# Last norm of a one-core transformer block: last quarter summed in PSUM, weights multiplied first, stores cut finer

## The chip, the cores and the metric

The kernel runs on one core of a Trainium2 chip. The metric is device time in microseconds from the start to the end of one execution; lower is better. Three runs of the kernel before took 734.03, 734.28 and 734.59, median 734.28.

## What is computed

A hybrid block on 512 rows of 1024 features: a norm, one wide projection, a gated linear attention branch and a latent attention branch, their gated sum through `w_out`, then a feed-forward part and a last norm. Only the end matters here:

```python
def rmsnorm(x, g):
    y = x * lax.rsqrt(jnp.mean(x * x, axis=-1, keepdims=True) + EPS)
    return y * g
...
m = rmsnorm(h, g_mlp)
h = h + jnp.square(jax.nn.relu(m @ w_ff1)) @ w_ff2     # 512x1024 -> 512x4096 -> 512x1024
return rmsnorm(h, g_final)
```

The output is 512 x 1024 in float32. Each row of the last norm needs the mean square of its whole row of h, so no row can leave before its last part of h is there.

## The kernel before

**Precision.** Every large product is made of three TensorE products: each factor is split into a high part, rounded by ScalarE (`AF.Copy` into a rounded float32 type), and a low part, the rest, which VectorE subtracts. Names end in h and l for the two: `g341h`, `g341l` are weights, `f3h`, `f3l` activations (helper `mm3`: high by high, low by high, high by low).

**Stages.** The feed-forward part runs in four quarters of the 4096 hidden features. Each quarter has a first product (`f0` to `f3`, with `w_ff1`) and a second (`g0` to `g3`, with `w_ff2`). Both are 2 x 2 block products made of seven block products instead of eight, numbered 1, 2, 5, 3, 6, 7, 4 in the order of the second kind. The 512 rows are four row tiles of 128; the tiles `h0` to `h3` (128 x 1024) hold the running h. In the second product, VectorE adds PSUM banks into them (`add_rows`, called by `sink`): `g3x0` and `g3x1` are the banks of blocks 1, 6 and 7 for the upper and lower row tile of a block, `g3z0` and `g3z1` those of 5 and 3. Block 7 adds onto the banks of block 6, so its first product into a bank waits until VectorE has read block 6 out of it.

**The end.** The last block, 4, adds only to the left halves of h2 and h3. `last_rows` makes it as `ge` (row tile 2, 512 columns, 12 products) and then, for row tile 3, as two quarters of 256 columns, `gend0` and `gend1` (12 products each). VectorE adds each into h. Around this the last norm of the four row tiles is made:

- the square of the right half and of the left half (or the two left quarters), on ScalarE, with a row sum into the small tile `hp` (columns 0 and 1); the squares themselves are written into the tile `ms` and not used;
- `out_mean` on GpSimd: sum times 1/D plus EPS; then on VectorE the other sum is added (`hp`, 128x1), and GpSimd takes the power -0.5 (`hp<-hp,mhalf`): this is the factor rs of a row;
- the right half: GpSimd multiplies h by the weights `gfin` into `ms` (`out_gained`), later ScalarE scales it by rs in place (`out_right`);
- the left half: VectorE does both in one instruction (`out_left`);
- `out_store`: two stores of 512 columns, all from the queue of SyncE but the very last, which ScalarE issues.

**What sets the order.** Steps of the earlier phases carry due times. From due time `base + 5700` on, everything is recorded instead of issued (`Held.hold`) and is then emitted in the order of the table `LAST_ROWS` (letter of the engine, tile written, count; P PE, A ScalarE, D VectorE, G GpSimd, S SyncE). Line 76 is where those instructions are emitted, line 90 where the others are; so rows of the end have line 76, and tiles tell them apart. Each engine works through its own queue in order. On GpSimd the queue of the end starts behind the loads of `w_ff2` pieces that it issues (`w<-in_w_ff`).

Of the kernel before, what the change touches and what calls it, by code (L numbers as in the profile page):

```python
# [11 lines left out]
F32 = mybir.dt.float32  # L12
F32R = mybir.dt.float32r
# [5 lines left out]
P = 128  # L19
# [78 lines left out]
def tile_block(ctx: ExitStack, tc: tile.TileContext, t, out: bass.AP):  # L98
# [1676 lines left out]
    def out_first(i):  # L1775
        hparts[i] = sm(f"hp{i}", 4)
        o = u4(f"ms{i}", F32, (P, D))
        ms_rows[i] = o
        nc.scalar.activation(o[:, 0:S], hrow[i][:, S:D], AF.Square, accum_out=hparts[i][:, 0:1])
# [5 lines left out]
    def out_gained(i):  # L1785
        nc.gpsimd.tensor_tensor(ms_rows[i][:, S:D], hrow[i][:, S:D], gains[0][:, S:D], op=ALU.mult)

    def out_square(i, cols, n=1):
        nc.scalar.activation(ms_rows[i][:, cols], hrow[i][:, cols], AF.Square, accum_out=hparts[i][:, n : n + 1])

    def out_rstd(i, n=1):
        p = hparts[i]
        nc.vector.scalar_tensor_tensor(
            p[:, 3:4], p[:, n : n + 1], 1.0 / D, p[:, 2:3], op0=ALU.mult, op1=ALU.add
        )
        nc.gpsimd.tensor_tensor(p[:, 3:4], p[:, 3:4], mhalf, op=ALU.pow)

    def out_left(i):
        o, rs = ms_rows[i], hparts[i][:, 3:4]
        nc.vector.scalar_tensor_tensor(o[:, 0:S], hrow[i][:, 0:S], rs, gains[0][:, 0:S], op0=ALU.mult, op1=ALU.mult)  # L1800

    def out_right(i):
        o, rs = ms_rows[i], hparts[i][:, 3:4]
        nc.scalar.activation(o[:, S:D], o[:, S:D], AF.Copy, scale=rs)

    def out_store(i):
        for c in range(2):
            cols = slice(c * S, (c + 1) * S)
            (nc.scalar if (i, c) == (3, 1) else nc.sync).dma_start(out[0, i * P : (i + 1) * P, cols], ms_rows[i][:, cols])

    def last_rows(ph):

        acc, parts = ps("mm", "ge"), (ps("mm", "gend0"), ps("at", "gend1"))
        cols = [slice(x * HT, (x + 1) * HT) for x in range(2)]

        def last_part(x):
            for p in range(NP):
                ph.second_product(4, parts[x][:, 0:HT], True, 1, p, cols[x])
            nc.vector.tensor_tensor(hrow[3][:, cols[x]], parts[x][:, 0:HT], hrow[3][:, cols[x]], op=ALU.add)

        for p in range(NP):
            ph.second_product(4, acc, True, 0, p)
        for i in (2, 3):
            out_first(i)
        out_mean(2)
        out_mean(3)
        out_gained(2)
        add_rows(2, 0, acc)
        out_square(2, slice(0, S))
# [303 lines left out]
```

## Time and profile before

| | us |
|---|---|
| median of three runs | 734.28 |
| the profiled execution | 733.97 |
| its span, first to last instruction | 732.2 |
| PE busy / VectorE / ScalarE / GpSimd | 723.8 / 624.6 / 494.4 / 223.2 |
| end of PE's last product (725.02 + 0.28) | 725.30 |
| end of the last scale on VectorE (727.48 + 0.75) | 728.23 |
| end of the span | 732.2 |

How to read it: rows of a timeline have the start in us from the begin of the span, the duration, the engine, the line, the operation, what is written and what is read (buffer numbers left out: `h` is any of h0 to h3), and shapes. A bracket at the end is the idle time before the row and who ended it. PE is TensorE, DVE VectorE, ACT ScalarE, POOL GpSimd, SP SyncE. A q behind an engine's name is its queue, as for the issue of a DMA. Matmuls are pipelined, so rows of PE overlap, and so do the first 0.08 us of a DVE row with the row before.

### The profile page before, as it was taken

Reading aid. Unit: us, or ns where it says so; the run is one execution under the profiler, and the core shown is the slowest. Engines: PE = TensorE matmul, PEld = TensorE weight load, DVE = VectorE, ACT = ScalarE, POOL = GpSimd, SP = SyncE. Lnnn points to the kernel's source line nnn. Section 1 sums busy time; section 2 is a strip of 40 time slices with the busy share of each in tenths; the row PEclk is TensorE's granted clock in tenths of the full one; section 3 lists DMA queues with packets and bytes.
Section 4 is the critical chain, followed back from the end, with each engine's and each line's share of the span. In section 5 each row is a group of like instructions: output and inputs, shape, how many; then the busy total and the mean of one; then the engine's idle time right before and its main releaser. Section 6 shows DMA issues by size and latency. Waiting matters only on the chain.

```text
span 732.2 us, 11361 instructions
## 1 busy us (share of the span) xinstructions
PE 723.8 (99%) x4150; PEld 637.6 (87%) x4150; DVE 624.6 (85%) x865; ACT 494.4 (68%) x810; POOL 223.2 (30%) x284
## 2 busy tenths in 40 slices
PE   9999999999999999999999999999999999999996
PEld 7888888888888888888888999889988998899985
DVE  7777887889988897789989789998699869987897
ACT  8556565595686864988867889545873477546855
POOL 0732020243843843226864412200211012101125
PEclk9999999999999999999999999999999999999998
DMA  9848682421222324657958899861987088815863
GB/s 311 279 137 194 214 179 89 82 64 29 58 59 59 90 45 114 180 160 190 246 87 218 188 214 202 177 211 61 249 182 195 11 240 189 199 59 143 173 99 131
DMA packets 81191, 109.93 MB, mean 150 GB/s; under 512 B 16208, under 2 KB 34640, under 8 KB 81136
## 3 DMA queue, kind: packets, MB, share of 16 engines
q1 hardware_dynamic: 63760, 75.64, 32.9%
q0 software_dynamic: 17088, 33.30, 27.5%
q8 instruction: 32, 0.52, 0.3%
q10 hardware_dynamic: 288, 0.28, 0.1%
q14 instruction: 23, 0.19, 0.1%
HBM read 104.22 MB, written 2.10 MB: 145 GB/s over the span
## 4 chain that ended last, share of the span: by engine, by line
PE 96%; DVE 2%; issue 1%; DMA 0%; ACT 0%; POOLq 0%; POOL 0%; DVEq 0%; ACTq 0%
PE f3x L90 3%; PE f2x L90 3%; PE f1x L90 3%; PE f0x L90 3%; PE first L90 3%; PE s L76 3%; PE av L76 3%; PE wox L76 3%; PE g2x L90 3%; PE g1x L90 3%; PE g0x L90 3%; PE gvx L90 3%; PE zax L90 3%; PE grx L90 3%; PE gk L90 2%; PE cq L90 2%
## 5 line engine op out<-in xcount | busy, mean ns | idle before, releaser
L90 POOL DMA_DIRECT2D w<-in_w_ff x32 | 38.6, 1205 | 240.1 <-DMA w<-in_w_ff 139.9
L76 ACT ACTIVATE e<-s,top 128x512 f32<-128x512 f32 x32 | 22.0, 689 | 8.5 <-DVE top L76 7.4
L76 DVE TENSOR_REDUCE top<-s 128x1 f32<-128x512 f32 x32 | 21.6, 685 | 5.9 <-PE s L76 5.6
L76 PE MATMUL s<-kbuf,q 96*128 96x512 f32 x96 | 26.6, 403 | 0.0
L76 PE MATMUL av<-pT,v 128*128 128x512 f32 (+1 forms) x108 | 25.4, 372 | 0.0
L76 DVE TENSOR_TENSOR pT<-tp,pT 128x512 fp32r<-128x512 f32 x32 | 21.7, 685 | 2.3 <-PE s L76 0.9
L76 ACT ACTIVATE pT<-tp 128x512 fp32r<-128x512 f32 x32 | 18.6, 599 | 5.9 <-PE tp L76 5.6
L76 PEld LDWEIGHTS av<-pT,v 128*128 128x128 f32 x108 | 18.6, 189 | 3.3
L76 PEld LDWEIGHTS s<-kbuf,q 96*128 96x128 f32 x96 | 17.0, 189 | 3.1 <-DVE grb L76 0.2
L76 PE MATMUL tp<-ident,e 128*128 128x128 f32 x128 | 17.9, 272 | 0.0
L76 PEld LDWEIGHTS tp<-ident,e 128*128 128x128 f32 x128 | 15.3, 140 | 2.7 <-ACT e L76 0.2
L90 POOL DMA_DIRECT2D gvw<-in_w_in x4 | 4.8, 1230 | 38.7 <-DVE gvw L90 34.0
L90 POOL TENSOR_TENSOR qF<-qk,qF 128x512 fp32r<-128x512 f32 x3 | 5.3, 1759 | 32.7 <-ACT qF L90 32.7
L90 POOL DMA_DIRECT2D zaw<-in_w_in x4 | 4.9, 1228 | 32.7 <-DVE zaw L90 28.0
L90 DVE TENSOR_TENSOR w<-w,w 128x1024 f32<-128x1024 f32 x12 | 14.4, 1221 | 0.1
L76 POOL DMA_DIRECT2D w<-in_w_ff x8 | 9.9, 1355 | 14.9 <-DVE g360l L76 7.0
L76 ACT ACTIVATE ms<-h 128x512 f32<-128x512 f32 (+1 forms) x17 | 10.2, 600 | 4.8 <-DVE h L76 4.7
L90 ACT ACT_TABLE_LOAD x9 | 11.5, 1283 | 1.2 <-PEq L2106 0.8
L76 POOL DMA_DIRECT2D w<-in_w_out x10 | 12.2, 1441 | 0.0
L76 POOL TENSOR_TENSOR my<-tb,yg 128x256 f32<-128x256 f32 x8 | 7.2, 898 | 13.7 <-DVE tb L76 7.5
L76 ACT ACTIVATE e<-e,tot 128x512 f32<-128x512 f32 x16 | 11.3, 720 | 0.0
L76 POOL TENSOR_TENSOR hp<-hp,mhalf 128x1 f32<-128x1 f32 x8 | 7.8, 980 | 8.9 <-DVE hp L76 8.7
(1954 smaller groups left out, 3084.2 us busy)
## 6 DMA issues: line engine op xcount, KB each, us to landing
w<-in_w_ff SPq DMA_DIRECT2D x48, 512.0 KB, 5.4
w<-in_w_ff POOLq DMA_DIRECT2D x40, 512.0 KB, 6.0
w<-in_w_out POOLq DMA_DIRECT2D x10, 512.0 KB, 5.9
grw<-in_w_in SPq DMA_DIRECT2D x8, 512.0 KB, 9.8
zaw<-in_w_in SPq DMA_DIRECT2D x8, 512.0 KB, 7.1
gvw<-in_w_in SPq DMA_DIRECT2D x8, 512.0 KB, 5.3
w<-in_w_out SPq DMA_DIRECT2D x16, 256.0 KB, 3.9
w221f<-in_w_ff SPq DMA_DIRECT2D x8, 512.0 KB, 5.2
```

The lines of the kernel that those rows point to most:

```text
L76: what(*args, **options)
L90: return what(*args, **options)
```

## The change

Four things, all in the last norm:

1. **The last quarter is summed in PSUM.** The right quarter of h3's left half is split into a high and a low part (`hend`, 128 x 2 x 256). Two products of an identity matrix (copied into `ones_r`, which is no longer needed as ones) add the two parts to `gend1`, after the sixth of its twelve products. VectorE's add into h is left out; the square reads the bank.
2. **The weights are multiplied first.** The left halves too get `h * gfin` first and are scaled by rs in place later: for row tiles 0 and 1 on GpSimd, for the two quarters of row tile 3 on VectorE, the last one from the bank. Row tile 2 keeps VectorE's one instruction for its left half.
3. **Who scales.** Left of row tile 0 is scaled by ScalarE, left of row tile 1 by VectorE, both without weights. Row tile 3 is cut at column 640: VectorE scales the 640 left columns, ScalarE the 384 right ones.
4. **Stores.** The right half of row tile 0 and both halves of row tile 1 leave as stores of 256 columns, row tile 3 as 640 and 384. Squares go to a scratch tile `junk`.

```diff
+    def out_begin(i):
+        if not spare:
+            spare.append(u2("junk"))
+            nc.scalar.activation(ones_r, ident, AF.Copy)
...
+    def out_gained(i, cols, eng=nc.gpsimd, src=None):
+        src = hrow[i][:, cols] if src is None else src
+        eng.tensor_tensor(ms_rows[i][:, cols], src, gains[0][:, cols], op=ALU.mult)
+
+    def out_scaled(i, cols, by_vector=False):
+        o, rs = ms_rows[i][:, cols], hparts[i][:, 3:4]
+        if by_vector:
+            nc.vector.tensor_scalar(o, o, rs, None, op0=ALU.mult)
+        else:
+            nc.scalar.activation(o, o, AF.Copy, scale=rs)
...
     def last_rows(ph):
...
+        split(rest[:, 0], rest[:, 1], hrow[3][:, QUARTERS[1]])
         add_rows(2, 0, acc)
...
+        for p in range(NP):
+            ph.second_product(4, last[0], True, 1, p, QUARTERS[0])
+        nc.vector.tensor_tensor(hrow[3][:, QUARTERS[0]], last[0], hrow[3][:, QUARTERS[0]], op=ALU.add)
         out_rstd(2)
+        out_square(3, hrow[3][:, QUARTERS[0]], 1)
+        out_gained(3, QUARTERS[0], nc.vector)
+        for p in range(NP):
+            ph.second_product(4, last[1], True, 1, p, QUARTERS[1])
+            if p == 1:
+                for x in range(2):
+                    nc.tensor.matmul(last[1], ones_r, rest[:, x], start=False, stop=False, skip_group_check=True)
...
+        out_added(3, 1, 2)
+        out_square(3, last[1], 0)
+        out_added(3, 0, 3)
+        out_gained(3, QUARTERS[1], nc.vector, last[1])
+        out_power(3)
+        cut = S + HT // 2
+        out_scaled(3, slice(0, cut), True)
+        out_scaled(3, slice(cut, D))
+        out_store(3, 0, cut)
+        out_store(3, cut, D, nc.scalar)
...
-        step(base + 7000 + i, out_first, i)
-        step(base + 7002 + i, out_mean, i)
-        step(base + 7002 + i, out_gained, i)
+        step(base + 7000 + i, out_begin, i)
+        step(base + 7002 + i, out_gained, i, LEFT)
...
-        A:g361h D:f3l60 P:g3z1*6 D:g361l A:g370h P:g3x1*3 D:f3l61 P:g3x0*3 A:f3h71 G:w2_21 A:f3h41 D:h0 P:g3x0*3
+        A:g361h D:f3l60 P:g3z1*6 D:g361l A:g370h P:g3x1*3 D:f3l61 P:g3x0*3 A:f3h71 G:w2_21 A:ones G:ms0 G:ms1 A:f3h41
```

On GpSimd, the queue behind its last weight load, up to the second row tile's power; `ms` is the tile that is stored, `hp` the small tile with the sums. Before:

```order
L76 DMA w2_21_736_2776<-in_w_ff2 128x2x512
L76 TENSOR_TENSOR ms0_1378_7482<-h0_869_2909,gfin_1330_7321 128x512
L76 TENSOR_SCALAR hp0_1377_7481<-hp0_1377_7481 128x1
L76 TENSOR_TENSOR hp0_1377_7481<-hp0_1377_7481,mhalf_74 128x1
L76 TENSOR_SCALAR hp1_1379_7483<-hp1_1379_7483 128x1
L76 TENSOR_TENSOR ms1_1380_7484<-h1_870_2910,gfin_1330_7321 128x512
L76 TENSOR_TENSOR hp1_1379_7483<-hp1_1379_7483,mhalf_74 128x1
```

And now:

```order
L76 DMA w2_21_736_2776<-in_w_ff2 128x2x512
L76 TENSOR_TENSOR ms0_1379_7483<-h0_869_2909,gfin_1330_7321 128x512
L76 TENSOR_TENSOR ms1_1381_7485<-h1_870_2910,gfin_1330_7321 128x512
L76 TENSOR_TENSOR ms0_1379_7483<-h0_869_2909,gfin_1330_7321 128x512
L76 TENSOR_SCALAR hp0_1378_7482<-hp0_1378_7482 128x1
L76 TENSOR_TENSOR hp0_1378_7482<-hp0_1378_7482,mhalf_74 128x1
L76 TENSOR_SCALAR hp1_1380_7484<-hp1_1380_7484 128x1
L76 TENSOR_TENSOR ms1_1381_7485<-h1_870_2910,gfin_1330_7321 128x512
```

The first two products of 128x512 are new (the left halves of row tiles 0 and 1); everything else stands behind them in the order of before. They wait for nothing later than the end of the `f3` products; the third waits for VectorE's add of block 6 into h0.

On VectorE, from the last split of weights to the end of the queue. Before:

```order
L76 TENSOR_TENSOR h3_872_2912<-h3_872_2912,g3x1_1329_7315 128x512 x2
L76 SCALAR_TENSOR_TENSOR ms0_1378_7482<-h0_869_2909,hp0_1377_7481,gfin_1330_7321 128x512
L76 TENSOR_TENSOR h2_871_2911<-h2_871_2911,ge_1381_7485 128x512
L76 SCALAR_TENSOR_TENSOR ms1_1380_7484<-h1_870_2910,hp1_1379_7483,gfin_1330_7321 128x512
L76 SCALAR_TENSOR_TENSOR hp2_1384_7488<-hp2_1384_7488 128x1
L76 TENSOR_TENSOR h3_872_2912<-gend0_1382_7486,h3_872_2912 128x256
L76 TENSOR_TENSOR h3_872_2912<-gend1_1383_7487,h3_872_2912 128x256
L76 SCALAR_TENSOR_TENSOR ms2_1385_7489<-h2_871_2911,hp2_1384_7488,gfin_1330_7321 128x512
L76 SCALAR_TENSOR_TENSOR hp3_1386_7490<-hp3_1386_7490 128x1 x2
L76 SCALAR_TENSOR_TENSOR ms3_1387_7491<-h3_872_2912,hp3_1386_7490,gfin_1330_7321 128x512
```

And now:

```order
L76 TENSOR_TENSOR h3_872_2912<-h3_872_2912,g3x1_1329_7315 128x512 x2
L76 TENSOR_SCALAR ms1_1381_7485<-ms1_1381_7485,hp1_1380_7484 128x512
L76 TENSOR_TENSOR h2_871_2911<-h2_871_2911,ge_1382_7486 128x512
L76 TENSOR_TENSOR hend_1385_7489<-h3_872_2912,hend_1385_7489 128x256
L76 TENSOR_TENSOR h3_872_2912<-gend0_1383_7487,h3_872_2912 128x256
L76 SCALAR_TENSOR_TENSOR hp2_1386_7490<-hp2_1386_7490 128x1
L76 TENSOR_TENSOR ms3_1389_7493<-h3_872_2912,gfin_1330_7321 128x256
L76 SCALAR_TENSOR_TENSOR ms2_1387_7491<-h2_871_2911,hp2_1386_7490,gfin_1330_7321 128x512
L76 SCALAR_TENSOR_TENSOR hp3_1388_7492<-hp3_1388_7492 128x1 x2
L76 TENSOR_TENSOR ms3_1389_7493<-gend1_1384_7488,gfin_1330_7321 128x256
L76 TENSOR_SCALAR ms3_1389_7493<-ms3_1389_7493,hp3_1388_7492 128x640
```

Row tile 1's left half became a scale, the low half of the split `hend` stands between the add of `ge` and that of `gend0`, and the add of `gend1` gave way to a product with the weights that stands behind the last mean.

On PE, around the place in the last quarter where the two identity products now stand (the same place held none before):

```order
L76 MATMUL gend1_1384_7488<-g340h_1373_7477,f3h40_1322_7295 128x256
L76 MATMUL gend1_1384_7488<-g340l_1374_7478,f3h40_1322_7295 128x256
L76 MATMUL gend1_1384_7488<-g340h_1373_7477,f3l40_1324_7297 128x256
L76 MATMUL gend1_1384_7488<-hend_1385_7489,ones_r_71 128x256 x2
L76 MATMUL gend1_1384_7488<-g341h_1375_7479,f3h41_1323_7296 128x256
L76 MATMUL gend1_1384_7488<-g341l_1376_7480,f3h41_1323_7296 128x256
```

The first of the two waits for ScalarE's high half of `hend`, the second for VectorE's low half; six products of the quarter stand ahead of them and six behind.

More of the change, by code (lines that the diff above doesn't have):

```diff
@@ L1795, in out_rstd, with out_power @@
         )
+    def out_power(i):
+        p = hparts[i]
         nc.gpsimd.tensor_tensor(p[:, 3:4], p[:, 3:4], mhalf, op=ALU.pow)
[L1798 to L1809, printed above, removed]
+    def out_rstd(i):
+        out_added(i, 1, 3)
+        out_power(i)
@@ L1811, in last_rows @@
     def last_rows(ph):
         acc, parts = ps("mm", "ge"), (ps("mm", "gend0"), ps("at", "gend1"))
[L1814 to L1819, printed above, removed]
+        rest = u2("hend", F32R, (P, 2, HT))
         for p in range(NP):
```

85 lines of the change are left out of this document (44 added, 41 removed).

## The prediction

> **What bounds the kernel now.** I read the profile from the whole to the end: first the busy times and the chain that ended last, then a table by stage of the last 18 us, then the rows of each engine there. The page says that TensorE is the bound:
>
> ```profile
> PE 723.8 (99%) x4150; PEld 637.6 (87%) x4150; DVE 624.6 (85%) x865; ACT 494.4 (68%) x810; POOL 223.2 (30%) x284
> PE 96%; DVE 2%; issue 1%; DMA 0%; ACT 0%; POOLq 0%; POOL 0%; DVEq 0%; ACTq 0%
> ```
>
> PE is busy for 723.8 of 732.2 us and is 96% of the chain. So an edit changes the time in two ways only: it makes PE's last product end earlier or later, or it changes what lies behind that product. Everything in the change sits behind 710 us, so the table by stage covers that stretch (us, then busy time of PE, weight loads, DVE, ACT, POOL, then the granted clock, the DMA share and GB/s):
>
> ```profile
> 714.00:721.00 7.00, 7.00 (x33) 5.79 (x32) 6.70 (x11) 5.32 (x13) 5.65 (x6) 1.00 0.22 40
> 721.00:725.30 4.30, 4.30 (x31) 3.86 (x29) 4.30 (x7) 2.06 (x5) 3.95 (x6) 1.00 0.27 100
> 725.30:728.30 3.00, 0.00 (x1) 0.00 (x0) 2.16 (x6) 2.24 (x6) 0.94 (x2) 0.90 0.88 326
> 728.30:732.20 3.90, 0.00 (x0) 0.00 (x0) 0.00 (x0) 0.00 (x0) 0.00 (x0) 0.50 0.47 178
> ```
>
> PE has no gap before 725.30. DVE has next to none either: 6.70 of 7.00 and 4.30 of 4.30. POOL has room only before 714. Behind PE stand 2.9 us of work on single row tiles and 3.9 us in which only DMA runs. The stage is therefore tight on two engines, and I need DVE's own rows (start, us, operands):
>
> ```profile
> 710.95 1.22 DVE L76 TENSOR_TENSOR g370l<-w,g370h 128x1024 fp32r<-128x1024 f32 x1
> 712.08 0.69 DVE L76 TENSOR_TENSOR f3l<-f3a,f3h 128x512 fp32r<-128x512 f32 x1
> 712.69 0.68 DVE L76 TENSOR_TENSOR h<-h,g3x 128x512 f32<-128x512 f32 x1
> 713.28 0.68 DVE L76 TENSOR_TENSOR f3l<-f3a,f3h 128x512 fp32r<-128x512 f32 x1
> 713.89 0.68 DVE L76 TENSOR_TENSOR h<-h,g3z 128x512 f32<-128x512 f32 x1
> 714.67 0.69 DVE L76 TENSOR_TENSOR h<-h,g3x 128x512 f32<-128x512 f32 x1
> 719.47 1.21 DVE L76 TENSOR_TENSOR g341l<-w,g341h 128x1024 fp32r<-128x1024 f32 x1
> 720.60 1.27 DVE L76 TENSOR_TENSOR h<-h,g3x 128x512 f32<-128x512 f32 x2
> 721.79 1.49 DVE L76 SCALAR_TENSOR_TENSOR ms<-h,hp,gfin 128x512 f32<-128x512 f32 x1
> 723.21 0.68 DVE L76 TENSOR_TENSOR h<-h,ge 128x512 f32<-128x512 f32 x1
> 724.98 0.78 DVE L76 TENSOR_TENSOR h<-gend,h 128x256 f32<-128x256 f32 x2
> 726.40 0.42 DVE L76 SCALAR_TENSOR_TENSOR hp<-hp 128x1 f32<-128x1 f32 x2
> 727.48 0.75 DVE L76 SCALAR_TENSOR_TENSOR ms<-h,hp,gfin 128x512 f32<-128x512 f32 x1 [0.66 <-POOL hp L76]
> ```
>
> PE's products that wait for them (the first onto g3x0 and onto g3x1 in the seventh block, the first that reads g341l, the seventh of the last quarter, the last):
>
> ```profile
> 714.11 0.39 PE L76 MATMUL g3x<-g370h,f3h 128*128 128x512 f32 x1
> 716.15 0.39 PE L76 MATMUL g3x<-g370h,f3h 128*128 128x512 f32 x1
> 721.14 0.39 PE L76 MATMUL ge<-g341l,f3h 128*128 128x512 f32 x1
> 724.42 0.28 PE L76 MATMUL gend<-g341h,f3h 128*128 128x256 f32 x1
> 725.02 0.28 PE L76 MATMUL gend<-g341h,f3l 128*128 128x256 f32 x1
> ```
>
> The margins are the core of the argument. The product at 714.11 may not write its bank before DVE has read it into h, which ends at 713.37: margin 0.74. The one at 716.15 needs the add that ends at 715.36: 0.79. The one at 721.14 needs g341l, done at 720.68: 0.46. So DVE may fall some 0.7 us behind before PE feels it, and later less.
>
> **The change part by part: the left products on GpSimd.** POOL gets two more products of 128x512 with both inputs in SBUF, first in its tail (lines out_gained of rows 0 and 1, left halves). Their data have long been there, so they start when the weight load issued at 710.13 leaves POOL:
>
> ```profile
> 710.13 1.21 POOL L76 DMA_DIRECT2D w<-in_w_ff  x1 [2.03 <-DVE g361l L76]
> 713.46 1.67 POOL L76 TENSOR_TENSOR ms<-h,gfin 128x512 f32<-128x512 f32 x1 [2.11 <-DVE h L76]
> 718.23 1.30 POOL L76 TENSOR_TENSOR ms<-h,gfin 128x512 f32<-128x512 f32 x1
> 719.62 1.46 POOL L76 TENSOR_TENSOR hp<-hp,mhalf 128x1 f32<-128x1 f32 x1
> 721.44 3.00 POOL L76 TENSOR_TENSOR ms<-h,gfin 128x512 f32<-128x512 f32 x2
> 726.90 0.55 POOL L76 TENSOR_TENSOR hp<-hp,mhalf 128x1 f32<-128x1 f32 x1 [1.21 <-DVE hp L76]
> ```
>
> No row of before shows these two instructions, so I price them from the nearest ones. Alone such a product takes 1.30 (718.23). The one at 713.46 took 1.67: it ended at 715.13, 1.16 after the DVE split with two SBUF inputs (713.28 to 713.97). The reverse is in DVE's row at 721.79: 1.49 instead of the 0.75 at 727.48, while POOL multiplied. An add from PSUM, 723.21, took its plain 0.68 beside POOL. So a DVE instruction with two SBUF inputs and a POOL product exclude each other, and one with a PSUM input is free. Who goes first when DVE has one such instruction behind another is seen earlier in the trace:
>
> ```profile
> 275.39 1.00 DVE L76 TENSOR_TENSOR ro<-roa,ro 128x512 fp32r<-128x512 f32 x1
> 275.80 1.19 POOL L76 TENSOR_TENSOR wk1l<-wk1f,wk1h 128x256 fp32r<-128x256 f32 x1
> 276.32 1.22 DVE L76 TENSOR_TENSOR ckvhl<-ckvc,ckvhl 128x512 fp32r<-128x512 f32 x1
> ```
>
> POOL waited from 275.80 for the first DVE instruction (end 276.39), went in between, ended at 276.99, and the second ended 0.55 later at 277.54. The Trainium skill, page "SBUF — State Buffer", section "Who interferes with whom", speaks against this part of the change: a GpSimd instruction and a Vector instruction with two SBUF inputs contend for a shared port pair, the later one is blocked whole, and issue order decides. By that rule the held split pays the full 1.16, and if the trace had shown Vector keeping the pair, the sum would be that of the first rival below; these rows agree with the rule.
>
> Now the steps. The left product of row 0 waits for g370l (end 712.17) and ends at 713.33. The first split behind it ends at 713.88 instead of 712.77, the add to h at 714.48 instead of 713.37, and PE's product of 714.11 starts near 714.5. The second left product waits for that split and ends at 715.04; the second split ends at 715.59 instead of 713.97. The two adds behind it took until 715.36, 1.39 after the split, so now 716.98, and PE's product of 716.15 starts near 717.0: **PE is 0.85 late**. The right product of row 0 then ends at 716.75, just ahead of the next split, and costs nothing. DVE was idle for 0.30 of the 7.00 us in this stage, 0.10 of it ahead of 714.67, so I let its lateness of 1.6 fall to 1.4: g341l ends at 722.1, PE wants it at 721.14 + 0.85 = 722.0. I count **+1.0** for this term. Its bounds are 0 (the margins swallow all) and 2 x 1.16 = 2.3 (both products arrive whole).
>
> **The identity products.** Two more products of 256 columns. The last quarter's rows stand 0.12 apart (724.42 to 725.02 in five steps), so **+0.24**; at the row's own 0.28 each it would be 0.56, and not below 0, as PE has no gap. The wait that comes with them: they need the low half of the split, and on DVE's queue that stands behind row 1's left scale and row 2's add, with the add of the other last quarter and row 2's mean queued behind it. At 1.4 late, h3's adds end at 723.3. POOL's product for row 2 starts behind the power, also 1.4 late, at about 722.85, and ends at 724.15. The scale is of this kind:
>
> ```profile
> 303.58 0.48 DVE L76 TENSOR_SCALAR e<-e,tot 128x512 f32<-128x512 f32 x1
> 331.64 1.64 DVE L76 TENSOR_SCALAR e<-e,tot 128x512 f32<-128x512 f32 x2
> 332.08 1.52 POOL L76 TENSOR_TENSOR wk3l<-wk3f,wk3h 128x256 fp32r<-128x256 f32 x2
> ```
>
> Alone 0.48, but 0.82 each beside POOL's products, so it is held too: end near 724.5. The add takes 0.6 more, POOL's row 3 product gets in (724.5 + 1.16 = 725.66), and the low half ends near 725.95. PE is at that place at 724.42 + 1.0 = 725.4. So the wait is between 0 and 0.5. I take **+0.2**, nearer to 0, because it needs every one of these turns to fall the late way.
>
> **Behind PE's last product.** Before, 725.30 to 728.23 is DVE's add (to 725.76), ScalarE's square with its accumulator, DVE's mean, POOL's power (726.90, 0.55) and the two scales:
>
> ```profile
> 725.90 0.40 ACT L76 ACTIVATE ms<-h 128x256 f32<-128x256 f32 x1
> 726.21 0.19 ACT L76 ACTIVATION_READ_ACCUMULATOR ms<-h 128x1 f32 x1
> 727.48 0.72 ACT L76 ACTIVATE ms<-ms,hp 128x512 f32<-128x512 f32 x1 [0.47 <-POOL hp L76]
> 728.23 0.38 ACTq L76 DMA_DIRECT2D out<-ms  x1
> ```
>
> The change takes the add away (0.46); the square reads PSUM itself and starts some 0.1 after PE, as it started 0.14 after the add before, so the rest up to the power is as long as it was. The scales shrink: DVE's from 0.75 to an estimated 0.55 for 640 columns (0.48 for 512, one SBUF input), ScalarE's from 0.72 to about 0.6 for 384, so 0.15 to 0.2. The gain of the last quarter by the weights, 0.42 on DVE, runs beside POOL's power of 0.55 and is hidden; without that cover it would cost 0.42. Together **-0.65**, between -0.4 (if row 2's left scale, held by its later power, delays the mean) and -0.7.
>
> **The rest at nothing.** Copying the identity into ones_r costs ScalarE one 128x128 copy, and ScalarE has room (busy 5.32 of 7.00 us). Squares go to a scratch tile, with the same instruction. Stores of rows 0 and 1 leave earlier and in quarters: SP does nothing else there. The DMA share is 0.27 before 725.30, so they find room; the last row's half megabyte still leaves after its scale and is moved in the last 3.9 us.
>
> Sum: 1.0 + 0.24 + 0.2 - 0.65 = +0.8. The profiled execution took 733.97 (span 732.2 and 1.8 around it), so 734.8; the median of the runs is 0.31 above it, 734.28, so **735.1**.
>
> **The rivals.** *The margins hold.* If POOL does not get between two DVE instructions, or DVE catches up, PE loses only the 0.24, and the sum is 0.24 - 0.65 = -0.4: 733.9. For it: margins of 0.74 and 0.79, and the 2.11 us that POOL idled before 713.46. Against: the rows at 275 to 277. *DVE becomes the bound.* The place is the low half of the split: if both products arrive whole (2.3) and the low half comes 0.5 after PE wants it, the sum is 2.3 + 0.24 + 0.5 - 0.65 = +2.4: 736.7, slower. It is over 0.2% from the point at which PE's last product ends later than 727.4, 2.1 us behind 725.30. For it: DVE is busy 4.30 of 4.30 us there and cannot catch up. Against: the adds from PSUM between the splits let POOL through. *The stores do more than I count.* If the earlier rows' bytes had held back the last ones, their early departure would be worth up to 0.25 more: with the first rival -0.65, 733.6. Against: the DMA share over the last 3.9 us is only 0.47.
>
> **How the numbers follow.** Forecast 0.52 (own range 734.4 to 735.8), margins hold 0.25, DVE becomes the bound 0.17, stores 0.06. A change of 0.2%, 1.47 us, is about what a measurement of this kernel can tell from none: below 732.81 is faster, above 735.75 slower. None of the cases but a tail of the last reaches faster: 0.02. The slow case and a tail of the forecast give slower 0.19; same 0.79. The range goes from 733.7, the margins case, to 736.4, most of the slow one.
>
> **What would show it.** In the changed profile I expect the first split after g370l to last about 1.8 us instead of 0.69, the second about 1.2; the POOL products before 715 about 1.9 and 1.75; PE gaps near 714.2 and 716.6 and its end near 726.7; from there to the last scale 2.3 us instead of 2.9. The prediction is wrong if both splits keep 0.69, if PE shows no gap before 719, or if a gap stands in front of the identity products that is longer than 0.5.

## The result, and the profile after

The changed kernel takes **737.42** us (median of 6 runs, 736.97 to 737.83); the kernel before took 734.28 beside it (6 runs, 733.89 to 734.79). The ratio is 1.0035, 95% interval 1.0024 to 1.0046: slower, by 3.1 us, and above the predicted range. The profiled execution took 737.32 with a span of 735.6.

The table by stage of the changed kernel, with the columns of before:

```profile
714.00:721.00 7.00, 4.93 (x22) 3.78 (x21) 6.70 (x9) 3.66 (x10) 3.54 (x4) 1.00 0.36 64
721.00:725.30 4.30, 4.30 (x20) 3.29 (x19) 4.30 (x8) 2.64 (x6) 3.90 (x5) 1.00 0.18 61
725.30:728.30 3.00, 3.00 (x23) 2.68 (x21) 3.00 (x5) 2.67 (x7) 2.89 (x3) 1.00 0.40 134
728.30:732.20 3.90, 1.12 (x8) 0.89 (x7) 2.71 (x9) 2.23 (x7) 1.36 (x3) 1.00 0.54 196
```

PE, full in the first stage before, is busy for 4.93 of 7.00 us, while DVE's 6.70 is what it was. PE lost 2.07 us in one wait; the list of waits (engine, what was waited for, us in total, times, longest) names it; three of its lines (PEld is PE's weight load):

```profile
PE g3x L76 <- DVE h L76: 2.1, 1, 2.1
PEld ge L76 <- DVE g341l L76: 0.4, 1, 0.4
PEld gend L76 <- DVE hend L76: 0.3, 1, 0.3
```

The rows there, of PE, DVE and POOL:

```profile
714.93 0.39 PE L76 MATMUL g3x<-g361h,f3l 128*128 128x512 f32 x1
717.39 0.47 PE L76 MATMUL g3x<-g370h,f3h 128*128 128x512 f32 x1 [2.07 <-DVE h L76]
...
711.99 4.05 DVE L76 TENSOR_TENSOR g370l<-w,g370h 128x1024 fp32r<-128x1024 f32 x1
715.97 0.68 DVE L76 TENSOR_TENSOR f3l<-f3a,f3h 128x512 fp32r<-128x512 f32 x1
716.57 0.67 DVE L76 TENSOR_TENSOR h<-h,g3x 128x512 f32<-128x512 f32 x1
717.17 0.68 DVE L76 TENSOR_TENSOR f3l<-f3a,f3h 128x512 fp32r<-128x512 f32 x1
...
711.18 1.21 POOL L76 DMA_DIRECT2D w<-in_w_ff  x1 [2.03 <-DVE g361l L76]
711.93 1.78 POOL L76 TENSOR_TENSOR ms<-h,gfin 128x512 f32<-128x512 f32 x1
713.18 1.77 POOL L76 TENSOR_TENSOR ms<-h,gfin 128x512 f32<-128x512 f32 x1
```

The last two rows are the left products; the second ends at 714.95. The weight split `g370l` lasted 4.05 instead of 1.22. It ended at 716.04, 1.09 after the second product, nearly all that it needs alone: it was kept out for both products, whole (1.22 is its row when nothing holds it). The two splits behind it kept 0.68. Everything behind it on DVE is 2.83 late; the margin of 0.74 from the prediction covers part, and 2.83 - 0.74 = 2.09 is PE's gap of 2.07.

**The books.** To compare profiles I take the start of the same PE product in each and in the profile of before (span 732.24). In us:

| kernel | late at 400 us | block 6, 7 | up to the last quarter | identity products | behind PE's end | span |
|---|---|---|---|---|---|---|
| before | 0 | 0 | 0 | - | 6.94 | 732.2 |
| changed | 1.05 | 2.34 | 0.25 | 0.56 | 6.12 | 735.6 |
| changed again (e13) | 2.41 | 3.96 | 0 | 0.22 | 5.74 | 737.6 |
| e1 no left products | 1.30 | 0 | 0 | 0.32 | 6.11 | 733.0 |
| e3 one left product | 0.73 | 1.08 | 0.24 | 0.59 | 6.11 | 734.0 |
| e9 no left, no identity | 0.55 | 0 | 0 | - | 6.50 | 732.3 |
| e10 products wait | 0 | 0.06 | 1.23 | 0.59 | 6.12 | 733.3 |
| e17 one product waits | 0.26 | 0.06 | 0.06 | 0.87 | 6.11 | 732.7 |

The second column is not the change's: it is lost in the first 9 us, by identical instructions, and differs from one execution to the next (last section). Without it the changed kernel is 2.34 + 0.25 + 0.56 - 0.82 = +2.33 in its first profile. The last 0.82 is a gain: from PE's end to the end of the span it takes 6.12 instead of 6.94.

### The profile page after: what moved, and what is told of

Read it like the earlier page. It is cut to its first block, busy times and chain, and to the rows that moved or that the text cites. A ratio compares the mean times of both kernels' runs of the same rounds, so it can differ in the third digit from the quotient of the medians.

```text
span 735.6 us, 11379 instructions
## 1 busy us (share of the span) xinstructions
PE 725.8 (99%) x4152; PEld 638.8 (87%) x4152; DVE 626.9 (85%) x866; ACT 495.7 (67%) x813; POOL 225.3 (31%) x286
## 4 chain that ended last, share of the span: by engine, by line
PE 96%; DVE 2%; issue 1%; DMA 0%; ACT 0%; POOL 0%; POOLq 0%; DVEq 0%
PE first L90 3%; PE f3x L90 3%; PE f2x L90 3%; PE f1x L90 3%; PE f0x L90 3%; PE s L76 3%; PE av L76 3%; PE wox L76 3%; PE g2x L90 3%; PE g1x L90 3%; PE g0x L90 3%; PE gvx L90 3%; PE zax L90 3%; PE grx L90 3%; PE gk L90 2%; PE cq L90 2%
## 5 line engine op out<-in xcount | busy, mean ns | idle before, releaser
L90 POOL DMA_DIRECT2D grw<-in_w_in x4 | 5.1, 1355 | 17.1 <-DVE gr60l L90 9.9
```

Source lines behind the costliest of these rows:

```text
L90: return what(*args, **options)
```

## The experiments

Theory 1 after the result: the left products on GpSimd cost nearly all of it, through `g370l`. Rivals: the identity products and VectorE's new order at the end. What then had to be explained is why one split waits for two products.

### Which part pays: e1, e2, e3

```diff
-        step(base + 7002 + i, out_gained, i, LEFT)         # e1; in e3 kept for i == 0
...
-                    nc.tensor.matmul(last[1], ones_r, rest[:, x], ...)         # e2
+        nc.vector.tensor_tensor(hrow[3][:, QUARTERS[1]], last[1], hrow[3][:, QUARTERS[1]], op=ALU.add)
```

**e1**, no left products; the left halves of row tiles 0 and 1 are scaled without the weights, so the kernel leaves out a part of the computation.

> The changed kernel without the two left products on GpSimd (the left halves of row tiles 0 and 1 are scaled without the weights, which is left out). Theory 1, GpSimd's two products shut VectorE's weight split out: g370l lasts 1.2 us instead of 4.05, TensorE's gap of 2.07 us ahead of the seventh block is gone, and the time is 0.3 to 0.7 us below the kernel before: 733.6 to 734.0. Rival, the cost sits in the identity products and in VectorE's longer queue at the end: the gap may go, but the time stays above 736. Rival, the slower first microseconds of the profiled run belong to the change: 734.7 to 735.1 at every run.

Measured: 734.91 (733.64 to 736.91), 1.0006 [0.9995, 1.0016]. `g370l` lasts 1.22, PE has no gap before the last quarter. The median is 0.9 above the top of what I expected; the profiled execution lost 1.30 at its start. Beside the books of the changed kernel the left products cost 2.33 - (0.32 - 0.83) = 2.84.

**e2**, the last quarter added on VectorE, the rest as changed.

> The changed kernel with the last quarter added on VectorE as before, everything else kept. Theory 1: the gap of 2.07 us ahead of the seventh block stays and the time is within 0.5 us of the changed kernel: 737.2 to 737.9, since the identity products' 0.24 and 0.33 of wait are given back and an add of 0.46 comes in. Rival, the identity products are the cost: under 736.

Measured: 737.17 (736.27 to 740.0), 1.0037 [1.0019, 1.0055]. `g370l` is 4.05 again. The identity products are not the cause of the gap.

**e3**, one left product (row tile 0); row tile 1's left half is scaled without the weights.

> The changed kernel with one left product on GpSimd, that of row tile 0 (row tile 1's left half is scaled without the weights). Theory 1: g370l waits for one product, lasts about 2.8 us instead of 4.05, TensorE's gap is about 0.85 us instead of 2.07, the time about 1.3 us below the changed kernel: 736.1. Rival, the weight load that GpSimd issues just ahead of the product holds VectorE, not the products: g370l stays above 3.5 us.

Measured: 735.65 (735.05 to 738.19), 1.0018 [1.0008, 1.0027]; `g370l` 2.81, PE's gap 0.83. One product holds the split for 1.59, two for 2.83.

### Why one split waits for both: e5, e6, e7

The prediction had the product wait for `g370l`. In the trace the product's row starts 0.06 ahead of the split's. That is little to go by: the same row starts 0.46 before the row of the load ahead of it ends (711.93, 712.39) and lasts 1.78, which is that 0.46 and the 1.30 of such a product alone. So a row's start on GpSimd need not be the start of its work. Theory A: who is first at what the two engines share has it, and the queue of GpSimd just keeps it. e5 put a memset of 128x512 ahead of the left products, so that the split would be ahead of them:

```diff
+            nc.gpsimd.memset(u2("pad"), 0.0)
-   G:w2_21 A:ones G:ms0 G:ms1
+   G:w2_21 A:ones G:pad G:ms0 G:ms1         # e5
+   G:w2_21 A:ones G:ms0 G:hp0 G:ms1         # e6: 128x1 between
+   D:g370l G:hp0 G:ms0 G:ms1                # e7: 128x1 that reads g370l, then the products
```

> The changed kernel with a memset of 128x512 on GpSimd between the weight load and the two left products, so that VectorE's g370l starts first. Theory 1a, GpSimd wins because its product starts 0.06 us ahead of g370l, and later the two engines take turns: g370l lasts 1.2 us, the splits behind it about 1.2 each at most, TensorE's gap is under 0.6 us, the time 734 to 735.5. Theory 1b, two products in a row keep VectorE out as a pair, wherever they start: some VectorE split lasts over 2.5 us and the time is 736.5 or more.

Measured: 737.55 (737.52 to 737.64), 1.0043 [1.0028, 1.0058]; `g370l` 4.51. The memset only lengthened the stay outside. It did not settle the order, because its own row too (711.01) starts ahead of the split's (711.10). Of the two expectations, the long hold came true (over 2.5, over 736.5).

> The changed kernel with one instruction of a single column (128x1, one operand in SBUF) put on GpSimd between the two left products; nothing else differs. Theory A, GpSimd keeps VectorE out for as long as its next instruction is ready, whatever that is: the split g370l still waits for both products and lasts about 4.2 us, TensorE's gap in front of block 7 is 2.1 to 2.3, and the time is 737.3 to 737.8. Theory B, VectorE waits for one product only and is kept out a second time because another large product stands right behind the first: with the small instruction between, g370l lasts about 2.8 as with a single left product, the second product waits for it and holds up one split behind it, the gap is about 0.8, and the time is 735.5 to 736.3.

Measured: 737.43 (737.13 to 739.87), 1.0036 [1.0024, 1.0047]; `g370l` 4.30, PE's gap 2.32. The small instruction ran in between and the split did not.

> The changed kernel with both left products moved on GpSimd behind a small instruction that reads one column of g370l, so that they can't start before that split is done: the order that the prediction assumed. If the forecast was wrong only in who goes first: g370l lasts 1.22, a split behind it about 1.8 and another about 1.2, TensorE stands 0.6 to 1.1 in front of a block 7 product, and the time is 735.2 to 736.0, as with one left product. If two products in a row also shut VectorE out here: one split behind g370l lasts 2.5 to 3.2, TensorE stands 1.3 to 2.3, and the time is 736.2 to 737.5.

Measured: 735.26 (735.06 to 737.08), 1.0007 [0.9997, 1.0017]. `g370l` 1.22, two later splits 1.40 and 1.66: here the engines take turns. The first of the two waits for the first left product, the second left product waits for that split, and the second split waits for the right product of row tile 0, which ends at 717.22. PE has no gap in block 7 and one of 0.91 in front of the product that reads `g341l`, which DVE now makes late.

### Who is first, or what stands ahead: e10, e14, e16, e18, e11

Theory C came up: what matters is that the products follow a weight load on GpSimd with no wait between. In e10 two instructions of one column stand ahead of the products, the second waiting for the first; e16 repeats it on two tiles, so that none waits; in e14 two VectorE instructions are exchanged and GpSimd's queue is the change's; e18 cuts the chain between the products; e11 moves the products behind the load before.

```diff
-   G:w2_21 A:ones G:ms0 G:ms1 A:f3h41  D:h0 P:g3x0*3 D:g370l P:g3x0*6
+   G:w2_21 A:ones G:hp0*2 G:ms0 G:ms1           # e10: hp0 column 3 twice
+   G:w2_21 A:ones G:hp0 G:hp1 G:ms0 G:ms1       # e16: no wait inside
+   G:w2_21 A:ones G:ms0 G:hp0*2 G:ms1           # e18
+   D:g370l P:g3x0*3 D:h0 P:g3x0*6               # e14
+   A:ones G:ms0 G:ms1 G:w2_21                   # e11
```

> The changed kernel with two instructions of one column (128x1, one operand in SBUF, about 0.2 us each) on GpSimd between the last weight load and the left products, so that the first product can start only after g370l has started. Theory A, whoever issues first holds the pair: g370l is now first, lasts 1.22, the products wait for it, and it goes as with the products behind the split: no gap in front of block 7, 735.2 to 735.8. Theory C, a chain of GpSimd instructions that follows a weight load without a wait keeps VectorE out from its first to its last instruction, however it begins: g370l lasts 4.4 to 4.7, TensorE stands 2.3 to 2.7 in front of block 7, and the time is 737.4 to 738.2.

Measured: 736.18 (735.54 to 737.78), 1.0018 [1.0006, 1.003]; span 733.3. The timeline of e10, DVE and POOL:

```profile
710.94 1.22 DVE L76 TENSOR_TENSOR g370l<-w,g370h 128x1024 fp32r<-128x1024 f32 x1
712.08 0.69 DVE L76 TENSOR_TENSOR f3l<-f3a,f3h 128x512 fp32r<-128x512 f32 x1
713.28 1.37 DVE L76 TENSOR_TENSOR f3l<-f3a,f3h 128x512 fp32r<-128x512 f32 x1
715.95 1.66 DVE L76 TENSOR_TENSOR f3l<-f3a,f3h 128x512 fp32r<-128x512 f32 x1
...
710.89 1.35 POOL L76 TENSOR_SCALAR hp<-mhalf 128x1 f32<-128x1 f32 x1
712.33 0.50 POOL L76 TENSOR_SCALAR hp<-mhalf 128x1 f32<-128x1 f32 x1
712.80 1.29 POOL L76 TENSOR_TENSOR ms<-h,gfin 128x512 f32<-128x512 f32 x1
714.07 1.74 POOL L76 TENSOR_TENSOR ms<-h,gfin 128x512 f32<-128x512 f32 x1
```

It looked like theory A: the split is unharmed, then turns. But the small row starts 0.05 ahead of the split (710.89), and it waited for it. The time lies between the two ranges.

> The changed kernel with two instructions of VectorE exchanged: the split g370l stands ahead of the addition h of row tile 0 instead of behind it, and so starts about 0.5 us ahead of the first left product instead of 0.06 behind it; GpSimd's order is the change's. Theory A, whoever is first at the pair decides, by however little: g370l lasts 1.22, VectorE and GpSimd then take turns, a later split or two last 1.4 to 1.8, no gap over 0.5 in front of block 7, and the time is 735.0 to 736.0. Theory C, two products that follow a weight load without a wait keep VectorE out once they run: g370l is past, but the next split behind it lasts 2.5 to 3.3, TensorE stands 1 to 2.3 us in block 7, and the time is 736.3 to 737.6.

Measured: 737.61 (737.26 to 738.38), 1.0040 [1.0027, 1.0054]. The timeline of e14:

```profile
711.59 4.65 DVE L76 TENSOR_TENSOR g370l<-w,g370h 128x1024 fp32r<-128x1024 f32 x1
...
711.37 1.21 POOL L76 DMA_DIRECT2D w<-in_w_ff  x1 [2.02 <-DVE g361l L76]
712.13 1.78 POOL L76 TENSOR_TENSOR ms<-h,gfin 128x512 f32<-128x512 f32 x1
713.38 1.77 POOL L76 TENSOR_TENSOR ms<-h,gfin 128x512 f32<-128x512 f32 x1
```

**Theory A falls here.** The split's row starts 0.54 ahead of the first product's, and still it ends 1.09 after the second one (716.24, 715.15). That the load, whose row starts 0.22 ahead of the split's, holds VectorE by itself is not what the traces show. In e1 the same split took 1.22 beside the end of the same load, and in the kernel before two VectorE instructions with both inputs in SBUF start 0.21 behind a load's row and take 1.29 together, no more than two such rows of 0.69 with the overlap of 0.08:

```profile
695.14 1.19 POOL L90 DMA_DIRECT2D w<-in_w_ff  x1 [6.41 <-DVE g350l L90]
695.35 1.29 DVE L90 TENSOR_TENSOR f3s<-f3s,f3a 128x512 f32<-128x512 f32 x2
```

Theory C had put the long wait on the split behind it, so its place was wrong too; that the chain keeps VectorE out stood. The Trainium skill, page "SBUF — State Buffer", section "Who interferes with whom", says that the order of issue decides which of the two engines is blocked. By these rows the first row on the timeline is not the one that goes first, and the loser can be kept out for more than one instruction; the rows decide.

> As e10, two instructions of one column on GpSimd between the last weight load and the left products, but on two different tiles, so that no instruction of GpSimd waits for the one ahead of it (in e10 the second waited for the first's end). Theory C, a chain that follows a weight load without a wait inside it keeps VectorE out to its end: g370l lasts 4.4 to 4.8, TensorE stands 2.4 to 2.8 in front of block 7, 737.4 to 738.4. Theory A', small instructions ahead let VectorE in first, wait or no wait: g370l lasts 1.2 to 1.4, then turns, 735.3 to 736.3 as in e10.

Measured: 737.52 (737.39 to 738.73), 1.0039 [1.0025, 1.0054]. The timeline of e16:

```profile
711.04 4.46 DVE L76 TENSOR_TENSOR g370l<-w,g370h 128x1024 fp32r<-128x1024 f32 x1
...
710.99 0.94 POOL L76 TENSOR_SCALAR hp<-mhalf 128x1 f32<-128x1 f32 x2
711.39 3.02 POOL L76 TENSOR_TENSOR ms<-h,gfin 128x512 f32<-128x512 f32 x2
```

Same small instructions, same place, without the wait inside: 4.46 instead of 1.22, although the first small row starts 0.05 ahead of the split in both. That is the cleanest pair of the study. **At this place the wait in GpSimd's queue decides, not the small instructions and not who starts first.**

> As e6, but with two instructions of one column between the left products, the second of which waits for the first's end, so that the chain behind the load is cut after the first product. Theory C: g370l waits for the first product alone and lasts 2.8 to 3.1 (two of these small ones can add 0.2 to 0.5 if VectorE is not let in before they end), the second product takes its turn behind it and holds up one later split by about 0.7; TensorE stands 0.8 to 1.3 in front of block 7, and the time is 735.8 to 736.8. If a cut in the chain makes no difference once the first product was ahead: 4.4 to 4.8 and 737.4 to 738.4 as in e6.

Measured: 736.48 (735.54 to 737.99), 1.0026 [1.0015, 1.0037]; span 733.9. The timeline of e18, VectorE and the first small instruction of GpSimd:

```profile
711.11 2.81 DVE L76 TENSOR_TENSOR g370l<-w,g370h 128x1024 fp32r<-128x1024 f32 x1
715.04 1.33 DVE L76 TENSOR_TENSOR f3l<-f3a,f3h 128x512 fp32r<-128x512 f32 x1
...
712.32 1.68 POOL L76 TENSOR_SCALAR hp<-mhalf 128x1 f32<-128x1 f32 x1
```

As theory C has it: cut behind the first product, the chain holds the split for one product (2.81, as in e3), and the second takes its turn (1.33). Beside e6 this is a second pair like e10 and e16: a small instruction at the same place behind the first product kept the split out where the next one was free to run (e6), and waited for it where the next one waits for the small one (e18: the split ends at 713.92, the small row at 714.00).

> The changed kernel with the two left products one place earlier on GpSimd, ahead of the last weight load instead of behind it: they then follow the load before it and start at about 707.7, beside f3l and g361l of block 6. Theory C, a chain behind a weight load keeps VectorE out to its end: the split f3l lasts about 3.2 instead of 0.68, TensorE stands 1 to 2 in block 6, not in block 7, and the time is 735.8 to 736.8. If VectorE gets its turn after one product at this place: f3l lasts 1.4 to 2.0, g361l 1.8, TensorE stands 0 to 0.8, and the time is 734.4 to 735.4.

Measured: 735.96 (735.6 to 738.5), 1.0019 [1.0006, 1.0032]. PE stands for 1.00 in block 6. The timeline of e11:

```profile
707.98 0.69 DVE L76 TENSOR_TENSOR f3l<-f3s,f3h 128x512 fp32r<-128x512 f32 x1
708.93 1.98 DVE L76 TENSOR_TENSOR g361l<-w,g361h 128x1024 fp32r<-128x1024 f32 x1 [0.25 <-ACT g361h L76]
710.84 1.77 DVE L76 TENSOR_TENSOR f3l<-f3s,f3h 128x512 fp32r<-128x512 f32 x1
...
707.99 1.84 POOL L76 TENSOR_TENSOR ms<-h,gfin 128x512 f32<-128x512 f32 x1
709.79 2.26 POOL L76 TENSOR_TENSOR ms<-h,gfin 128x512 f32<-128x512 f32 x1
```

Also behind a load, also no wait: and yet turns. The splits (1.98 and 1.77) are close to those of the second possibility; only the time and PE's gap fit theory C. So theory C as I wrote it is too wide. One difference is seen in POOL's rows: in the changed kernel and in e14 the second product's row starts 0.53 ahead of the first one's end (713.18 and 711.93 + 1.78 = 713.71), here 0.04 ahead (709.79 and 709.83), in e10 0.02. Another is that the first product of e11 was itself held: it ended 1.16 after the split `f3l` (708.67). But an overlap of rows is not the rule either: in e18 the first small row starts 0.51 ahead of the product's end (712.32, 712.83), and VectorE went in there. Nor is it enough that the next instruction has to wait: behind the one left product of e3 stands a product that waits for VectorE, and the split was held for that one all the same. **What decides between a held chain and turns stays open.** Shown are the two pairs (e10 and e16, e18 and e6), in which a wait inside the chain made the difference, and e11, where a chain without a wait took turns at another place. Whether the load ahead has a part in it, once products follow, was not tried by itself.

### Can the gains be kept? e8, e9, e12, e15, e17, e19

All but e9 compute everything. **e8**: no left products; VectorE scales and weights the left halves of row tiles 0 and 1 in one instruction each, as before, with `hend` split earlier and row tile 2's left half moved behind the last sums of squares.

```diff
-        out_scaled(1, LEFT, True)
+        out_left(1)         # scalar_tensor_tensor(h, rs, gfin); the same for row tile 0
...
-        step(base + 7002 + i, out_gained, i, LEFT)
```

> The whole computation, with the identity products and the store pieces of the change, but no left products on GpSimd: the left halves of row tiles 0 and 1 are scaled and weighted in one VectorE instruction each, as in the kernel before; the high and low half of hend come ahead of them on ScalarE and VectorE, and row tile 2's left half goes behind the last sums of squares. If the left products are what the change pays for: no gap in front of block 7, the wait in front of the identity products (0.31 without left products) is gone, and the time is 733.9 to 734.6, just under the kernel before. If VectorE's two longer instructions (1.2 to 1.5 each beside GpSimd's products) come back at the end: 734.9 to 735.6.

Measured: 735.77 (735.25 to 737.03), 1.0018 [1.0009, 1.0026]. PE ended only 0.22 later than before plus the start, but 7.59 lay behind it. One of the two instructions took 1.77 beside GpSimd's products; VectorE is the bound at the end, as the second possibility said. A part of it, about 0.25, is row tile 2's left half: its row (728.76 to 729.50) stands ahead of the last scale, whose factor was ready at 729.14.

**e9** leaves out the left products and the identity products (left halves of row tiles 0 and 1 without the weights), with VectorE's add as in e2.

> No left products on GpSimd and no identity products: the last quarter is added on VectorE as in the kernel before; the order of the last steps and the store pieces are those of the change. The left halves of row tiles 0 and 1 are scaled without the weights. If the identity products gain at the end what they were made for, this kernel ends 0.2 to 0.6 later than the same one with them (734.91): 735.1 to 735.5. If their wait for the low half of hend (0.31) and their own 0.24 eat that: 734.5 to 735.0.

Measured: 734.47 (733.36 to 735.82), 0.9995 [0.9985, 1.0004]; the first possibility did not come, the time is just under the range of the second. Set against e1 this prices the identity products: they shorten the stretch behind PE from 6.50 to 6.11, a gain of 0.39, and cost PE 0.22 where nothing waits (e13), 0.32 in e1, and 0.56 to 0.87 where `hend` is late. So they are worth 0.07 in e1 and lose where `hend` is late, as in the first profile of the change (0.39 against 0.56). The rest of the change's end (order, scales, stores) gains 6.94 - 6.50 = 0.44; e2, which computes everything, has the same 6.50.

**e12**: the kernel before with only the last cut at column 640 and row tile 3's left half weighted ahead.

```diff
+        nc.vector.tensor_tensor(o[:, 0:S], hrow[3][:, 0:S], gains[0][:, 0:S], op=ALU.mult)
...
-        out_left(3)
-        out_right(3)
-        out_store(3)
...
+        nc.vector.tensor_scalar(o[:, 0:cut], o[:, 0:cut], rs, None, op0=ALU.mult)
+        nc.scalar.activation(o[:, cut:D], o[:, cut:D], AF.Copy, scale=rs)
...
```

> The kernel before with only the last step of the change: row tile 3's left half is multiplied with the weights on VectorE while it waits for the factor, the last scaling and the last store are cut at column 640 instead of 512 (VectorE 640 columns, ScalarE 384). Whole computation, no left products on GpSimd, no identity products, the order before as it was. The last scaling is 0.55 and 0.62 instead of 0.75 and 0.72 and the smaller last store lands earlier: 0.3 to 0.5 less than the kernel before, 734.2 to 734.5 where that has 734.8. If the added product (0.68, two operands in SBUF) meets GpSimd's power of row tile 3 and delays it: 734.8 to 735.3.

Measured: 734.61 (733.88 to 736.34), 0.9994 [0.9984, 1.0003]; 7.01 behind PE, no gain. GpSimd's power took 0.93 instead of 0.55 beside the added product (512 columns, both inputs in SBUF), which gives back what the cut gains:

```profile
726.82 0.93 POOL L76 TENSOR_TENSOR hp<-hp,mhalf 128x1 f32<-128x1 f32 x1 [1.21 <-DVE hp L76]
```

**e15** is e14 with one left product and `out_left(1)`; **e17** is e10 with one left product and `out_left(1)`; **e19** is e17 with the identity products behind the ninth product instead of the sixth (`if p == 2`).

> The whole computation: the change with the same exchange on VectorE, only row tile 0's left product on GpSimd, and row tile 1's left half scaled and weighted in one VectorE instruction as in the kernel before. If a single product that takes its turn costs VectorE 0.7 to 0.8 and TensorE's margin covers half of it, and the VectorE instruction is 0 to 0.3 longer than the scaling that it replaces (1.23): 734.3 to 735.0, level with the kernel before or just under it. If the product still stands ahead of a split, or the longer instruction comes back at the end in full: 735.2 to 736.0.

Measured: 736.85 (736.57 to 738.73), 1.0039 [1.0026, 1.0052]. A miss: in e14's order one product holds `g370l` too (3.41).

> The whole computation: the change with e10's two small instructions (the second waits for the first) ahead of row tile 0's left product, and row tile 1's left half scaled and weighted in one VectorE instruction. One product that takes its turn costs VectorE about 0.7, of which TensorE's margin should cover most: no gap over 0.4 on TensorE, against the kernel before 0 to +0.6 us: 734.5 to 735.3. If the margin does not cover it, or the VectorE instruction comes back at the end: 735.5 to 736.2.

Measured: 734.36 (734.07 to 737.06), 1.0000 [0.9991, 1.0009]. The change with one of its two left products, and a wait ahead of it, is level with the kernel before, just under the expected range. Left over is the wait for `hend`, of which this row shows a part (0.87 lost there, 0.22 of it the products' own):

```profile
725.47 0.39 PE L76 MATMUL gend<-hend,ones_r 128*128 128x256 f32 x1 [0.37 <-DVE hend L76]
```

> As e17 (whole computation), with the two identity products three products later on TensorE, where the low half of hend has had 0.36 us more: the wait in front of them, 0.67 in e17, becomes 0.3, and if the time behind TensorE's last product stays as it was, this kernel ends 0.3 to 0.4 ahead of e17: 734.0 to 734.2 where the kernel before has 734.5. If VectorE is what the end waits for by then, nothing is gained: 734.3 to 734.7.

Measured: 734.81 (734.15 to 735.81), 1.0003 [0.9994, 1.0012]. PE gains 0.37 (0.87 to 0.50) and the stretch behind it grows by 0.37 (6.11 to 6.48). The second possibility came true, with a time 0.1 above its range: VectorE's and GpSimd's chain of means and powers sets the end (row tile 3's last mean stands on VectorE behind row tile 2's left half, which waits 0.44 for GpSimd's power). No version that I ran beats the kernel before by more than its runs can tell.

### The same kernel again: e13

> The changed kernel once more, unaltered, for a second profile and more times beside the other experiments. If the start of the program costs a different time in each execution (in the profiles so far TensorE's first products ran at half pitch for 0 to 2.4 us longer than in the kernel before), its offset in the first 9 us differs from 1.09 while the gap in front of block 7 stays 2.0 to 2.4; if it belongs to the change, it is 1.0 to 1.2 again. The half pitch of 3.4 us behind the gap, which two experiments showed and the first profile of the change did not, comes or stays away with the same gap. Time 736.9 to 738.0 either way.

Measured: 737.46 (736.8 to 739.34), 1.0036 [1.0023, 1.0049]. The gap of 2.07 is there again, to the hundredth. The start cost 2.41 instead of 1.05 with the same kernel, so it belongs to the execution and not to the change. And this time PE ran at half pitch behind the gap (last section).

## Why the prediction was wrong

**What bounds it** and **the margins** held. PE's first product of block 7 waits for the add that the margin of 0.74 was read from, and 2.09 came out where the row shows 2.07.

**The step that failed**: "The left product of row 0 waits for g370l (end 712.17) and ends at 713.33." It did not wait. The product's row began 0.06 ahead of the split's, and the split waited for both products (4.05). The quoted step took its data from rows at 275 us, where one GpSimd product goes in between two VectorE instructions; I carried the turn over to a chain of two products that stands behind a load. e16 beside e10 shows that a wait in GpSimd's queue can decide which of the two happens; why the engines behave so stays open. With it fell what hung on it: the two splits kept 0.68, PE's gap stands in one place, and the term of +1.0 was 2.34 + 0.25 = 2.59. My upper bound for the term, both products whole at 2.3, was near but too low; I gave that case 0.17. The rival with it, +2.4, lies close to the +2.33 of the profile, but in part by luck: it put the place at the low half of `hend`, where PE waited for 0.34 only.

What the rest was worth is seen in e10, where VectorE's split goes first as the prediction assumed, though the products start 0.6 later than it had them. The first split behind `g370l` kept 0.69 (1.8 predicted), the next took 1.37 (1.2 predicted), and a third took 1.66, because row tile 0's right product stood in front of it until 717.07. The prediction had that product end "just ahead of the next split" and cost nothing, so this reading fails there too. The term is 0.06 + 1.23 = 1.29 (1.0), and the whole 733.3 - 732.2 = +1.1 where the forecast's sum was +0.8. PE's lateness came out not in block 7, where 0.85 was predicted, but in front of `g341l`, whose margin of 0.46 was smaller.

**Identity products**: +0.24 was 0.22. Their wait, +0.2, was 0.34 (0.56 - 0.22): within the 0 to 0.5 given.

**Behind PE's last product**: -0.65 was -0.82, a little beyond the bound of -0.7. The identity products bring 0.39 of it, which is less than the add of 0.46 taken away; the rest, 0.44, comes from scales, order and stores together, which were not taken apart. The power of 0.55 did cover the last product with the weights, as I had counted: in the changed kernel it kept 0.55 beside that product, which reads the bank. In e12, where the product reads SBUF alone, it did not.

**The sum and the median.** The sum from the first profile is +2.33 and the medians differ by 3.1. The first profile is the mild one: in five of seven profiles with a gap of 2 us or more PE then lost another 1.7 at half pitch. I had no term for that. In e13, the same kernel, the sum with it is 3.96 + 0.22 - 1.20 = +2.98, only 0.65 more than +2.33, because a later PE no longer waits for `g341l` and `hend` and has less behind it (5.74). Which of the six runs had it is not shown, as one was profiled. I also started from a profile of before whose start happened to cost nothing.

## What to carry to other kernels

Before you move work to an engine that shares a resource, look at what stands ahead of it in its queue: the same two products made PE 2.6 us late right behind a load and 1.3 behind a short wait, with the same data at the same place. A turn-taking pattern read from single instructions elsewhere in a trace need not hold for a chain. And when PE's last product and the work behind it are both tight, what is taken out of one comes back in the other (e19), so price them together.

## What the runs showed of the hardware

**The start.** PE's first products run at half pitch for a time that changes with each execution. The second group in the changed kernel, which starts 0.43 ahead of the next one, and the same one before, 0.23 ahead:

```profile
5.05 0.63 PE L90 MATMUL first<-xT,first0l 128*128 128x256 f32 x2
```

```profile
4.79 0.40 PE L90 MATMUL first<-xT,first0l 128*128 128x256 f32 x2
```

Over 20 profiles it cost between 0 and 2.7 us against the profile of before, with identical instructions: nearly as much as the 3.1 under study. Medians of few runs carry it; terms were therefore read from profiles.

**Half pitch behind a gap.** In e13, behind the gap of 2.07, PE's timeline and the table by stage (0.70 is the granted clock):

```profile
719.53 0.54 PE L76 MATMUL g3x<-g370h,f3h 128*128 128x512 f32 x1
719.88 0.63 PE L76 MATMUL g3x<-g370l,f3h 128*128 128x512 f32 x1
720.30 0.63 PE L76 MATMUL g3x<-g370h,f3l 128*128 128x512 f32 x1
720.73 0.63 PE L76 MATMUL g3x<-g371h,f3h 128*128 128x512 f32 x1
```

```profile
718.00:722.00 4.00, 3.24 (x9) 2.56 (x10) 3.70 (x8) 3.29 (x8) 2.21 (x3) 0.70 0.00 0
```

Eight rows (719.88 to 722.86) stand 0.43 apart instead of 0.23, and 1.7 us are lost, which is half of 3.4. It came in e2, e5, e6, e13 and e16 (gaps of 2.07 to 2.54) and not in the first profile of the change (2.07) nor in e14 (2.67): the length of the gap does not decide alone. The Trainium skill, page "TensorE: Matmul & The Clock Gate", section "Part 1: The HAM clock gate", has a window of about 3.4 us that runs free of the kernel, after which an idle PE is halved; the 3.4 us and the chance in it agree with these rows, but here a gap of 2.07, shorter than a window, was enough.
